# State-space x, B and C of groups 1 to 3: from tokens as the stationary operand to weights as the stationary operand

## The chip, the core and the metric

The kernel runs on one core of one Trainium2 chip. TensorE (PE) multiplies, VectorE (DVE), ScalarE (ACT) and GpSimd (POOL) work on tiles in SBUF and on accumulators in PSUM, and DMA queues (SP's and POOL's here) bring weights in. The metric is the device time of one execution in microseconds (us). The kernel before takes 2125.59 us, the median of three runs from 2124.63 to 2127.35. The profiled execution took 2124.81 us and its span, first to last instruction, is 2122.9 us.

## The reference

Four layers work on 256 tokens of 1024 features. Each layer is a feed-forward block, a mixer, and a second feed-forward block, with a layer norm after each. The mixer of layers 0 and 3 is a state-space one (`mamba2_mixer`); layers 1 and 2 have attention. The part that matters:

```python
def mamba2_mixer(x, w_in, conv_w, conv_b, ...):
    zxbcdt = x @ w_in
    z, xbc, dt = jnp.split(zxbcdt, [SSM_D_INNER, SSM_D_INNER + SSM_CONV_DIM], axis=-1)
    xbc = lax.conv_general_dilated(xbc, conv_w[:, None, :], ..., feature_group_count=SSM_CONV_DIM) + conv_b
    xbc = jax.nn.silu(xbc)
    xs, b_ssm, c_ssm = jnp.split(xbc, [SSM_D_INNER, SSM_D_INNER + G * N], axis=-1)
```

So `x` (2048 features), `B` and `C` (512 each) are projected, go through a convolution of four taps along the tokens, separate for each feature, and through SiLU. There are four groups; a group has 512 features of x, 128 of B and 128 of C, which is 768 features or six blocks of 128.

## The kernel before

The tokens stand in two tiles of 128, t = 0 and t = 1. Each has its own generator (`stream`, inside it `ffn`, `ssm` or `attn`), and the driver at the end of `build` steps them by turns: tile 1 runs two pieces behind tile 0 (`lag_at`, `LAG`). A piece is one block of weights of at most 128 x 2048 numbers, one MB. `fetch` brings it into one of 3 `raw` buffers by SP's queue, `load` splits it into a high half `wh` (ACT, L159) and the rest `wl` (DVE, L160), four instructions of 512 columns on each engine, into one of 5 buffers each. A buffer comes free when the second of the tiles has used its piece.

A product is made of three matmuls (`mm3`, L187, L190, L191): high x high, high x low, low x high. The stationary operand is a 128 x 128 block of the layer's input, transposed and split (`xh`, `xl`, made by `to_T`), and the moving operand is 512 or 256 columns of the weights. So a result stands with tokens on the partitions.

In the state-space mixer the pieces go in the order `SSM_ORDER`: X0, Z0, X1, Z1, O0, X2, Z2, X3, O1, Z3, O2, O3. X is x, B and C of a group, Z its gate, O the output projection. X1, X2 and X3 have three pieces: two with 512 columns of x for half of the 1024 inputs each (`proj512`), one with the 256 columns of B and C (`proj256`). Both tiles multiply every piece. The convolution needs features on the partitions, so `stage_x` copies the result from PSUM to SBUF (ACT, L480), transposes four blocks on PE (`transposes`, L199), and copies them into `xb` (DVE, L482); `stage_bc` does it with two blocks (L492, L199, L494). When tile 1 has done so, `conv` runs for both tiles: on ACT the first tap with the bias (L457), on DVE three taps (L461), on ACT SiLU (L464). `stage_back` then turns x back (L504), scales it (DVE, L509), multiplies C by B (L518) and masks the product (DVE, L521); `stage_off` multiplies by the earlier tile's states (L527), `stage_m` makes the decays on ACT (L540, L541) with a product on DVE (L542), `stage_y` multiplies (L550), `stage_z` is the gate's SiLU (L559). SiLU and the exponential need different function tables on ACT, which ACT_TABLE_LOAD brings in.

The instructions are written in this order, but a scheduler (the Tile layer) reorders them by priority, by when it thinks their operands ready, and by free buffers; `keep_in_program_order` and `high_priority` steer it. PSUM has 8 banks: two each for the tags `acc0`, `acc1`, `gu` (`G`) and `tp` (`T`). Up to the first O piece the projections use `acc0` and `acc1` (`GA`), later ones `gu`, which the products of L527 and L550 use too.

Of the kernel before, what the change touches and what calls it, by code (L numbers as in the profile page):

```python
# [16 lines left out]
S = 256  # L17
# [60 lines left out]
def build(tc, x, wst, ln_g, ln_b, sm_rows, sm_conv, sm_nw, fx_b, out, plan=None):  # L78
# [28 lines left out]

    ident = cpool.tile([128, 128], F32, name="ident")
# [95 lines left out]
    def to_T(st, h):  # L204
        xh = spool.tile([128, KT, 128], FR, name=f"xh{st.t}", bufs=1)
        xl = spool.tile([128, KT, 128], FR, name=f"xl{st.t}", bufs=1)
        for half in range(2):
            tp = transposes(h[:, half * 512:half * 512 + 512], 4)
            sl = slice(half * 4, half * 4 + 4)
            for ins in split(tp.rearrange("p (a b) -> p a b", a=4), xh[:, sl], xl[:, sl]):  # L210
                if opening:
                    tc.keep_in_program_order(ins)
        st.xh, st.xl = xh, xl
# [51 lines left out]
    def proj256(st, ps, w):  # L265
        wh, wl = w
        for k in range(KT):
            mm3(ps[:, :256], st.xh[:, k], st.xl[:, k], wh[:, k * 256:(k + 1) * 256], wl[:, k * 256:(k + 1) * 256],
                k == 0, k == KT - 1)

# [141 lines left out]
    def ssm(st, j):  # L412
# [56 lines left out]
        def frame(g):  # L469
            if t == 0:  # L470
                s.xb[g] = spool.tile([128, 6, S + 3], F32, name="xb", tag="t4", bufs=2)
                s.cv[g] = spool.tile([128, 6, S], F32, name="cv", tag="t4", bufs=2)
                nc.gpsimd.memset(s.xb[g][:, :, 0:3], 0.0)

        def stage_x(g):
            if g:
                frame(g)
            n = 4 if g else 3
            xc = tmp(512, "t2", 4)
            nc.scalar.activation(xc[:, :n * 128], bank.pop(g)[:, :n * 128], AF.Copy)  # L480
            tp = transposes(xc, n)
            nc.vector.tensor_copy(s.xb[g][:, 0:n, 3 + t * 128:131 + t * 128],  # L482
                                  tp[:, :n * 128].rearrange("p (a b) -> p a b", a=n))
            if t == 1:
                conv(g, 0, 4)

        def stage_bc(g):
            if g == 0:
                frame(g)
            n = 2 if g else 3  # L490
            bcs = tmp(128 * n, "t1", 5) if g else tmp(512, "t2", 4)[:, :384]
            nc.scalar.activation(bcs, bank.pop(g if g else "b")[:, :n * 128], AF.Copy)  # L492
            tp = transposes(bcs, n)
            nc.vector.tensor_copy(s.xb[g][:, 6 - n:6, 3 + t * 128:131 + t * 128],  # L494
                                  tp[:, :n * 128].rearrange("p (a b) -> p a b", a=n))
            if t == 1:
                conv(g, 4, 6)
# [85 lines left out]
        for g in range(N_GRP):  # L583
            b = where["X", g, 2 if g else 3]
            at(b - 1 if g else b, stage_x, g)
            at(b if g else 1, stage_bc, g)
# [15 lines left out]
        for i, (kind, g, n) in enumerate(pieces):  # L602
            if kind == "X" and g == 0:
                if n % 2 == 0:
                    ps = bank["b" if n == 0 else 0] = GA(int(n == 0))
            elif (kind == "X" and n != 1) or (kind == "Z" and n == 0):
                ps = bank[g] = GA(int(kind == "Z" or n == 2)) if i < first_o else G()
# [3 lines left out]
            elif kind == "X" and g == 0:  # L611
                proj512(st, ps, n % 2, w, 416 if n < 2 else 384)
            elif kind == "X" and n == 2:
                proj256(st, ps, w)
            else:
                proj512(st, ps, n, w)
            for f, a in post.get(i, ()):
# [284 lines left out]
def pack_ssm(w_in, w_out):  # L902
    P = []
    dn = rows2(w_out)
    for it in SSM_ORDER:
# [5 lines left out]
        elif it[0] == "X":  # L911
            P += cols512(w_in[:, 2048 + g * 512:2048 + (g + 1) * 512])
# [80 lines left out]
```

## Time and profile before

| what | before |
|---|---|
| median of three runs | 2125.59 us (2124.63 to 2127.35) |
| profiled execution | 2124.81 us, span 2122.9 us |
| PE busy | 2099.0 us (99%), 10218 matmuls |
| PE's weight loads (PEld) busy | 1735.6 us (82%), 10218 |
| DVE, ACT, POOL busy | 1461.4 (69%), 1177.0 (55%), 480.9 us (23%) |
| TensorE's granted clock | 0.999 of full speed |

How to read it: a matmul's row is longer than the distance to the next one, since matmuls overlap. What a matmul costs is therefore read from the distance between starts, and what PE waits from the gaps that a row names in brackets. The two state-space mixers stand at about 194 to 364 us and 1736 to 1908 us.

### The profile page before, as it was taken

The page shows a single profiled execution, that of the slowest core. Times are in us where ns is not written, and L with a number is a line of the kernel's source. Part 1 is how long each engine was busy: PE and PEld are TensorE (multiplying, and loading weights), DVE is VectorE, ACT ScalarE, POOL GpSimd, SP SyncE. Part 2 cuts the span into 40 slices and gives each one's busy share as a digit, 9 for nine tenths or more (in the row PEclk, how much of TensorE's full clock was granted, in tenths as well). Part 3 has the DMA queues.
Part 4 walks back from the last instruction along what each step waited for, and adds up shares of the span by engine and source line. Part 5 has one row for each costly group of instructions (what it writes and reads, how often), then busy time and mean ns, then how long its engine had stood idle before and what let it go on. Part 6 is the DMA issues. An engine that isn't in the chain of part 4 may idle for free.

```text
span 2122.9 us, 29645 instructions
## 1 busy us (share of the span) xinstructions
PE 2099.0 (99%) x10218; PEld 1735.6 (82%) x10218; DVE 1461.4 (69%) x2829; ACT 1177.0 (55%) x2453; POOL 480.9 (23%) x871
## 2 busy tenths in 40 slices
PE   8999999999999999999999999999999999999998
PEld 7888878888888888788888888788888888788886
DVE  6557888855765585766675575765575578888565
ACT  5545997544544455544444455544445449975442
POOL 2331000233143210043233300034223310002331
PEclk9999999999999999999999999999999999999999
DMA  9665654666576653476566653376666656446662
GB/s 316 224 229 203 215 171 172 217 232 224 189 256 227 224 201 122 165 235 230 204 245 230 222 193 139 123 247 238 225 221 232 221 205 220 173 161 221 230 227 95
DMA packets 227559, 441.72 MB, mean 208 GB/s; under 512 B 20752, under 2 KB 21072, under 8 KB 227408
## 3 DMA queue, kind: packets, MB, share of 16 engines
q1 hardware_dynamic: 198768, 397.73, 52.5%
q0 software_dynamic: 28640, 42.09, 6.8%
q8 instruction: 80, 1.31, 0.3%
q14 instruction: 71, 0.58, 0.1%
HBM read 417.61 MB, written 22.13 MB: 207 GB/s over the span
## 4 chain that ended last, share of the span: by engine, by line
PE 91%; DVE 4%; ACT 2%; DMA 1%; issue 1%; POOL 0%; SPq 0%; DVEq 0%; ACTq 0%
PE gu L187 16%; PE gu L190 16%; PE gu L191 16%; PE acc L191 9%; PE acc L187 9%; PE acc L190 9%; PE ga L187 3%; PE ga L190 3%; PE ga L191 3%; PE tp L199 3%; DVE wl L160 2%; PE gu L550 1%; DMA raw<-in_w_dram 1%; PE gu L747 1%; DVE cv L461 1%
## 5 line engine op out<-in xcount | busy, mean ns | idle before, releaser
L160 DVE TENSOR_TENSOR wl<-raw,wh 128x512 fp32r<-128x512 f32 (+1 forms) x1412 | 889.1, 680 | 363.1 <-ACT wh L159 361.7
L159 ACT ACTIVATE wh<-raw 128x512 fp32r<-128x512 f32 (+1 forms) x1412 | 778.8, 620 | 511.2 <-PE gu L191 230.0
L187 PE MATMUL gu<-wh,xh 128*128 128x512 f32 (+1 forms) x1600 | 619.4, 387 | 2.7 <-ACT wh L159 1.2
L190 PE MATMUL gu<-wl,xh 128*128 128x512 f32 (+1 forms) x1600 | 618.6, 387 | 0.0
L191 PE MATMUL gu<-wh,xl 128*128 128x512 f32 (+1 forms) x1600 | 618.1, 386 | 0.0
L291 POOL DMA_DIRECT2D aT<-turn x640 | 348.3, 551 | 488.4 <-issue 314.7
L187 PEld LDWEIGHTS gu<-wh,xh 128*128 128x128 f32 x1600 | 301.1, 188 | 65.0 <-ACT wh L159 2.0
L187 PE MATMUL acc<-wh,ah 128*128 128x512 f32 x896 | 352.7, 394 | 0.0
L191 PE MATMUL acc<-wh,al 128*128 128x512 f32 x896 | 351.9, 393 | 0.3 <-DVE al L160 0.3
L190 PE MATMUL acc<-wl,ah 128*128 128x512 f32 x896 | 351.5, 392 | 0.0
L190 PEld LDWEIGHTS gu<-wl,xh 128*128 128x128 f32 x1600 | 301.2, 188 | 60.5 <-DVE wl L160 1.0
L191 PEld LDWEIGHTS gu<-wh,xl 128*128 128x128 f32 x1600 | 301.2, 188 | 59.8 <-DVE xl L160 0.4
L315 ACT ACTIVATE t<-gu 128x256 f32<-128x256 f32 x176 | 67.5, 383 | 267.8 <-PE gu L191 247.2
L317 DVE TENSOR_TENSOR t<-t,gu 128x256 f32<-128x256 f32 x176 | 73.4, 417 | 189.6 <-ACT t L315 189.6
L191 PEld LDWEIGHTS acc<-wh,al 128*128 128x128 f32 x896 | 168.3, 188 | 36.5 <-DVE al L160 2.1
L187 PEld LDWEIGHTS acc<-wh,ah 128*128 128x128 f32 x896 | 168.3, 188 | 35.8 <-issue 1.3
L190 PEld LDWEIGHTS acc<-wl,ah 128*128 128x128 f32 x896 | 168.3, 188 | 34.5 <-issue 1.3
L287 POOL DMA_DIRECT2D turn<-tb x160 | 90.4, 565 | 330.9 <-DVE tb L285 298.5
L187 PE MATMUL ga<-wh,xh 128*128 128x512 f32 (+4 forms) x448 | 159.5, 357 | 0.4 <-ACT xh L159 0.4
L190 PE MATMUL ga<-wl,xh 128*128 128x512 f32 (+4 forms) x448 | 156.8, 351 | 0.0
L191 PE MATMUL ga<-wh,xl 128*128 128x512 f32 (+4 forms) x448 | 155.7, 349 | 0.0
L235 POOL TENSOR_TENSOR rstd<-ve,mhalf 128x1 f32<-128x1 f32 x24 | 22.7, 945 | 441.9 <-DVE ve L233 441.9
(181 smaller groups left out, 1655.5 us busy)
## 6 DMA issues: line engine op xcount, KB each, us to landing
raw<-in_w_dram SPq DMA_DIRECT2D x354, 1024.0 KB, 5.3
turn<-tb POOLq DMA_DIRECT2D x160, 128.0 KB, 3.1
aT<-turn POOLq DMA_DIRECT2D x640, 32.0 KB, 3.9
mt<-cums SPq DMA_DIRECT2D x32, 256.0 KB, 4.2
gb<-in_ln_g_dram SPq DMA_DIRECT2D x12, 512.0 KB, 4.7
gb<-in_ln_b_dram SPq DMA_DIRECT2D x12, 512.0 KB, 5.8
nw<-in_sm_nw_dram SPq DMA_DIRECT2D x8, 256.0 KB, 5.4
h<-in_x_dram SPq DMA_DIRECT2D x4, 256.0 KB, 4.9
```

The lines of the kernel that those rows point to most:

```text
L159: a = nc.scalar.activation(wh, raw, AF.Copy)
L160: return a, nc.vector.tensor_sub(wl, raw, wh.bitcast(F32))
L187: first = nc.tensor.matmul(o, xh, wh, start=start, stop=False)
L190: nc.tensor.matmul(o, xh, wl, start=False, stop=False)
L191: nc.tensor.matmul(o, xl, wh, start=False, stop=stop)
L199: ins = nc.tensor.transpose(tp[:, j * 128:(j + 1) * 128], src[:, j * 128:(j + 1) * 128], ident)
L235: nc.gpsimd.tensor_tensor(rstd, ve, mhalf, op=ALU.pow)
L287: nc.gpsimd.dma_start(dr, b.rearrange("p q k t -> p (q k t)"))
L291: nc.gpsimd.dma_start(aT[32 * q:32 * q + 32].rearrange("p i k t -> p i (k t)"), dv[q])
L315: nc.scalar.activation(sg, gu[:, :256], AF.Silu)
L317: nc.vector.tensor_mul(a, sg, gu[:, 256:])
L461: nc.vector.scalar_tensor_tensor(cv[:, i], xb[:, i, k:k + S], w[:, k:k + 1], cv[:, i], op0=ALU.mult, op1=ALU.add)
```

## The change

For groups 1 to 3 the operands change places. A piece now holds 256 features for all 1024 inputs: two pieces of x and one of B and C per group. `proj_T` takes a 128 x 128 block of the weights as the stationary operand and the 256 tokens of both tiles as the moving one. For this the four tensors `xh0`, `xl0`, `xh1`, `xl1` become slices of one constant tile `x4`, in which the high halves of both tiles stand side by side and the low halves too. The result comes out with features on the partitions and all tokens in a row, so `stage_T` copies it from PSUM straight into `xb` (ACT) and `conv` follows for two blocks at a time. Tile 0 does nothing in these pieces; tile 1 does the whole, at its own place in the order, two pieces behind. Group 0 stays as it was.

```diff
+    x4 = cpool.tile([128, KT, 4, 128], FR, name="x4")
...
     def to_T(st, h):
-        xh = spool.tile([128, KT, 128], FR, name=f"xh{st.t}", bufs=1)
-        xl = spool.tile([128, KT, 128], FR, name=f"xl{st.t}", bufs=1)
+        xh, xl = x4[:, :, st.t], x4[:, :, 2 + st.t]
...
+    def proj_T(ps, w):
+
+        wh, wl = w
+        for f in range(2):
+            o = ps[:, f * S:f * S + S]
+            for k in range(KT):
+                sl = slice(k * 256 + f * 128, k * 256 + f * 128 + 128)
+                nc.tensor.matmul(o, wh[:, sl], x4[:, k, 0:2], start=k == 0, stop=False, skip_group_check=True)
+                nc.tensor.matmul(o, wh[:, sl], x4[:, k, 2:4], start=False, stop=False, skip_group_check=True)
+                nc.tensor.matmul(o, wl[:, sl], x4[:, k, 0:2], start=False, stop=k == KT - 1, skip_group_check=True)
...
         def frame(g):
-            if t == 0:
+            if t == 0 or g:
...
-            n = 4 if g else 3
-            xc = tmp(512, "t2", 4)
-            nc.scalar.activation(xc[:, :n * 128], bank.pop(g)[:, :n * 128], AF.Copy)
-            tp = transposes(xc, n)
-            nc.vector.tensor_copy(s.xb[g][:, 0:n, 3 + t * 128:131 + t * 128],
-                                  tp[:, :n * 128].rearrange("p (a b) -> p a b", a=n))
-            if t == 1:
-                conv(g, 0, 4)
...
+        def stage_T(g, n):
+
+            if n == 0:
                 frame(g)
...
+            nc.scalar.activation(s.xb[g][:, 2 * n:2 * n + 2, 3:3 + S],
+                                 bank.pop((g, n)).rearrange("p (a b) -> p a b", a=2), AF.Copy)
+            conv(g, 2 * n, 2 * n + 2)
...
         for g in range(N_GRP):
             b = where["X", g, 2 if g else 3]
-            at(b - 1 if g else b, stage_x, g)
-            at(b if g else 1, stage_bc, g)
+            if g == 0:
+                at(b, stage_x)
+                at(1, stage_bc)
+            elif t == 1:
+                for n in range(3):
+                    at(b - 2 + n, stage_T, g, n)
...
-            elif kind == "X" and n == 2:
-                proj256(st, ps, w)
-            else:
+            elif kind == "Z":
                 proj512(st, ps, n, w)
+            elif t == 1:
+                ps = bank[g, n] = GA(0) if i < first_o else G()
+                proj_T(ps, w)
...
         elif it[0] == "X":
-            P += cols512(w_in[:, 2048 + g * 512:2048 + (g + 1) * 512])
+            for n in (0, 256):
+                P += cols256(w_in[:, 2048 + g * 512 + n:2048 + g * 512 + n + 256])
```

What the scheduler makes of it is seen in the order of the instructions. Line numbers after the change are a little higher: L279 to L281 are `proj_T`, L189, L192 and L193 are `mm3`, L201 and L519 transposes, L533 is L518 of before, L542 is L527, L161 is the split's high half, L469 and L476 belong to `conv`, L510 is the copy of `stage_T`, L555 and L556 are `stage_m`, and L574 is the gate's SiLU.

First place: PE in the first state-space mixer, where the last piece of X1 (B and C) is multiplied. `tp<-ident,t` are transposes into PSUM, x4 counts four of them. Before:

```order
L191 MATMUL ga<-wh,xl_1935 128x256
L187 MATMUL ga<-wh,xh_1934 128x256
L190 MATMUL ga<-wl,xh_1934 128x256
L191 MATMUL ga<-wh,xl_1935 128x256
L199 MATMUL tp<-ident,t_2484 128x128 x4
L187 MATMUL ga<-wh,xh_1934 128x256
L190 MATMUL ga<-wl,xh_1934 128x256
```

The same place after the change:

```order
L279 MATMUL ga<-x_78,wh 128x256
L280 MATMUL ga<-x_78,wh 128x256
L281 MATMUL ga<-x_78,wl 128x256
L279 MATMUL ga<-x_78,wh 128x256
L280 MATMUL ga<-x_78,wh 128x256
L281 MATMUL ga<-x_78,wl 128x256
L189 MATMUL acc_2617<-wh,ah 128x512
```

The transposes of x and of B and C are gone from PE (36 in each of the two mixers), and the piece runs into the output projection O0; a group's 96 matmuls of both tiles, half of them of 512 and half of 256 columns, have become 144 of 256.

Second place: PE in the first mixer where the output projection O1 begins (`acc`). `tp<-cv` is the product of C and B of group 2, and L527 the product with the earlier states. Before:

```order
L191 MATMUL gu<-wh,xh_1934 128x512
L187 MATMUL gu<-wh,xh_1934 128x512
L190 MATMUL gu<-wl,xh_1934 128x512
L199 MATMUL tp<-ident,t_3175 128x128 x4
L191 MATMUL gu<-wh,xl_1935 128x512
L527 MATMUL gu<-xe,t_3130 128x512
L187 MATMUL acc_2602<-wh,ah 128x512
L190 MATMUL acc_2602<-wl,ah 128x512
L191 MATMUL acc_2602<-wh,al 128x512
```

After:

```order
L189 MATMUL gu<-wh,x_78 128x512
L192 MATMUL gu<-wl,x_78 128x512
L193 MATMUL gu<-wh,x_78 128x512
L189 MATMUL acc_2617<-wh,ah 128x512
L189 MATMUL acc_2762<-wh,ah 128x512
L189 MATMUL acc_2618<-wh,ah 128x512
L189 MATMUL acc_2763<-wh,ah 128x512
L192 MATMUL acc_2617<-wl,ah 128x512
L533 MATMUL tp<-cv 128x128
L519 MATMUL tp<-ident,cv 128x128 x4
```

O1 now begins ahead of the product of C and B, directly behind the gate projection Z2 of tile 1, and its first matmuls are those of both tiles that need only the high halves of the weights; X3, which was multiplied by tile 0 ahead of O1, now follows it.

Third place: ACT in the same stretch. `wh_3134` and `wh_3206` before, `wh_3158` and `wh_3205` after, are the two pieces of O1; `mt` belongs to the decays, `t2` of L559 or L574 to the gate. Before:

```order
L540 ACTIVATE mt_3552<-mt_3552,ncum_2095 128x128
L159 ACTIVATE wh_3134<-raw_3132 128x512 x2
L464 ACT_TABLE_LOAD
L464 ACTIVATE cv_2828<-cv_2828 128x512
L159 ACTIVATE wh_3134<-raw_3132 128x512 x2
L480 ACTIVATE t2_3175<-gu_3026 128x512
L540 ACTIVATE mt_3552<-mt_3552,ncum_2095 128x128 x2
L541 ACT_TABLE_LOAD
L541 ACTIVATE mt_3552<-mt_3552 128x512
L159 ACTIVATE wh_3206<-raw_3204 128x512 x4
L559 ACT_TABLE_LOAD
L559 ACTIVATE t2_3201<-gu_3066 128x512
```

After:

```order
L161 ACTIVATE wh_3105<-raw_3103 128x512 x3
L161 ACTIVATE wh_3158<-raw_3156 128x512 x2
L476 ACT_TABLE_LOAD
L476 ACTIVATE cv_2922<-cv_2922 128x512
L161 ACTIVATE wh_3158<-raw_3156 128x512 x2
L161 ACTIVATE wh_3205<-raw_3203 128x512 x4
L555 ACTIVATE mt_3291<-mt_3291,ncum_2153 128x128 x3
L555 ACTIVATE mt_3611<-mt_3611,ncum_2088 128x128
L556 ACT_TABLE_LOAD
L556 ACTIVATE mt_3291<-mt_3291 128x512
L574 ACT_TABLE_LOAD
L574 ACTIVATE t2_3201<-gu_3102 128x512
```

The splits of O1's two pieces stand closer together, and the gate's SiLU (L574), after which the `gu` bank of the first piece of X3 comes free, stands behind them and behind two table loads. In the whole program the ACT_TABLE_LOADs go from 57 to 61, two more in each mixer. Outside the two mixers the order on every engine is what it was.

## Rows read from the trace of the kernel before

**Rows 1.** The page's first part: busy time of each engine, share of the span and instructions.

```profile
PE 2099.0 (99%) x10218; PEld 1735.6 (82%) x10218; DVE 1461.4 (69%) x2829; ACT 1177.0 (55%) x2453; POOL 480.9 (23%) x871
```

**Rows 2.** The page's fourth part: the chain that ended last, by engine.

```profile
PE 91%; DVE 4%; ACT 2%; DMA 1%; issue 1%; POOL 0%; SPq 0%; DVEq 0%; ACTq 0%
```

**Rows 3.** Busy time in stretches of the first mixer, of a feed-forward block and of the second mixer (us from the span's start; PE, PEld, DVE, ACT, POOL busy with their instructions, granted clock, DMA share, GB/s).

```profile
220.00:320.00 100.00, 97.22 (x542) 82.26 (x541) 87.41 (x178) 97.50 (x196) 3.09 (x7) 1.00 0.55 189
400.00:570.00 170.00, 170.00 (x752) 140.25 (x752) 105.94 (x200) 81.12 (x169) 54.73 (x100) 1.00 0.67 231
1763.00:1863.00 100.00, 97.21 (x543) 82.02 (x542) 87.34 (x175) 97.50 (x195) 3.10 (x7) 1.00 0.54 187
```

**Rows 4.** What PE waited for in the first mixer, 193.86 to 364 us: who waited, for whom, us in total, times, longest. In the second, 1736.5 to 1908 us, the same rows stand without the one of L492.

```profile
PE tp L518 <- ACT cv L464: 1.2, 1, 1.2
PE gu L527 <- DVE t L521: 1.1, 1, 1.1
PE tp L199 <- ACT t L492: 1.0, 1, 1.0
PE gu L187 <- ACT t L559: 0.6, 1, 0.6
PE tp L199 <- DVE t L569: 0.4, 1, 0.4
```

**Rows 5.** Timeline of PE, matmuls of 512 columns: start us, length, instruction. First and last of 25 in an unbroken run.

```profile
184.76 0.40 PE L187 MATMUL acc<-wh,ah 128*128 128x512 f32 x1
...
190.22 0.39 PE L187 MATMUL acc<-wh,ah 128*128 128x512 f32 x1
```

**Rows 6.** The same view, matmuls of 256 columns, first, two in the middle and last of 21; and of 272 columns, first and last of 24.

```profile
290.24 0.28 PE L187 MATMUL gu<-wh,xh 128*128 128x256 f32 x1
290.36 0.28 PE L190 MATMUL gu<-wl,xh 128*128 128x256 f32 x1
...
292.63 0.28 PE L191 MATMUL gu<-wh,xl 128*128 128x256 f32 x1
...
756.85 0.28 PE L187 MATMUL ga<-wh,xh 128*128 128x272 f32 x1
...
759.74 0.29 PE L191 MATMUL ga<-wh,xl 128*128 128x272 f32 x1
```

**Rows 7.** The same view: four transposes among matmuls of 256 columns, and two among matmuls of 512.

```profile
255.99 0.28 PE L191 MATMUL ga<-wh,xl 128*128 128x256 f32 x1
256.11 0.60 PE L199 MATMUL tp<-ident,t 128*128 128x128 f32 x4
256.47 0.37 PE L187 MATMUL ga<-wh,xh 128*128 128x256 f32 x1
256.67 0.28 PE L190 MATMUL ga<-wl,xh 128*128 128x256 f32 x1
...
245.10 0.39 PE L190 MATMUL ga<-wl,xh 128*128 128x512 f32 x1
245.33 0.38 PE L199 MATMUL tp<-ident,t 128*128 128x128 f32 x2
245.47 0.48 PE L191 MATMUL ga<-wh,xl 128*128 128x512 f32 x1
245.78 0.39 PE L187 MATMUL ga<-wh,xh 128*128 128x512 f32 x1
```

**Rows 8.** Timeline of PE's weight loads in the stretch of Rows 6: the load that belongs to its second matmul.

```profile
290.24 0.19 PEld L190 LDWEIGHTS gu<-wl,xh 128*128 128x128 f32 x1
```

**Rows 9.** Groups of ACT's and DVE's instructions in the first mixer: line, engine, operation, out<-in, shapes, count | busy us, mean ns of one | idle before.

```profile
L541 ACT ACT_TABLE_LOAD x9 | 11.5, 1283 | 0.2
...
L480 ACT ACTIVATE t<-gu 128x512 f32<-128x512 f32 x4 | 2.3, 581 | 0.3 <-PE gu L191 0.3
L492 ACT ACTIVATE t<-gu 128x256 f32<-128x256 f32 x4 | 1.5, 377 | 2.5 <-PE gu L191 2.5
...
L482 DVE COPY xb<-tp 128x512 f32<-128x512 f32 x6 | 4.1, 684 | 1.1 <-PE tp L199 1.1
L494 DVE COPY xb<-tp 128x256 f32<-128x256 f32 x6 | 2.5, 418 | 0.1
```

**Rows 10.** Timeline of ACT, and of PE, around PE's longest wait in the first mixer.

```profile
269.69 1.28 ACT L541 ACT_TABLE_LOAD   x1
...
271.63 1.28 ACT L464 ACT_TABLE_LOAD   x1
272.93 0.63 ACT L464 ACTIVATE cv<-cv 128x512 f32<-128x512 f32 x1
...
273.61 0.49 PE L518 MATMUL tp<-cv 128*128 128x128 f32 x2 [1.16 <-ACT cv L464]
```

**Rows 11.** Timeline of ACT in the stretch where X3 begins, with the four parts of a split and four first taps of the convolution in a row.

```profile
302.39 2.18 ACT L159 ACTIVATE wh<-raw 128x512 fp32r<-128x512 f32 x4
304.47 2.07 ACT L457 ACTIVATE cv<-xb,conv 128x256 f32<-128x256 f32 x4
306.56 1.28 ACT L559 ACT_TABLE_LOAD   x1
307.86 0.60 ACT L559 ACTIVATE t<-gu 128x512 f32<-128x512 f32 x1
308.35 0.62 ACT L464 ACTIVATE cv<-cv 128x512 f32<-128x512 f32 x1
```

More of the change, by code (lines that the diff above doesn't have):

```diff
@@ L473, in frame, with stage_x, stage_bc @@
                 nc.gpsimd.memset(s.xb[g][:, :, 0:3], 0.0)
-        def stage_x(g):
-            if g:
-                frame(g)
-            n = 4 if g else 3
-            xc = tmp(512, "t2", 4)
-            nc.scalar.activation(xc[:, :n * 128], bank.pop(g)[:, :n * 128], AF.Copy)
-            tp = transposes(xc, n)
-            nc.vector.tensor_copy(s.xb[g][:, 0:n, 3 + t * 128:131 + t * 128],
-                                  tp[:, :n * 128].rearrange("p (a b) -> p a b", a=n))
-            if t == 1:
-                conv(g, 0, 4)
[L487 to L497, printed above, removed]
+        def stage_x():
+            xc = tmp(512, "t2", 4)
+            nc.scalar.activation(xc[:, :384], bank.pop(0)[:, :384], AF.Copy)
+            tp = transposes(xc, 3)
+            nc.vector.tensor_copy(s.xb[0][:, 0:3, 3 + t * 128:131 + t * 128],
+                                  tp[:, :384].rearrange("p (a b) -> p a b", a=3))
+            if t == 1:
+                conv(0, 0, 4)
+        def stage_bc():
+            frame(0)
+            bcs = tmp(512, "t2", 4)[:, :384]
+            nc.scalar.activation(bcs, bank.pop("b")[:, :384], AF.Copy)
+            tp = transposes(bcs, 3)
+            nc.vector.tensor_copy(s.xb[0][:, 3:6, 3 + t * 128:131 + t * 128],
+                                  tp[:, :384].rearrange("p (a b) -> p a b", a=3))
+            if t == 1:
+                conv(0, 4, 6)
+        def stage_T(g, n):
+            if n == 0:
+                frame(g)
+            nc.scalar.activation(s.xb[g][:, 2 * n:2 * n + 2, 3:3 + S],
+                                 bank.pop((g, n)).rearrange("p (a b) -> p a b", a=2), AF.Copy)
+            conv(g, 2 * n, 2 * n + 2)
         def stage_back(g):
@@ L605, in ssm @@
                     ps = bank["b" if n == 0 else 0] = GA(int(n == 0))
-            elif (kind == "X" and n != 1) or (kind == "Z" and n == 0):
-                ps = bank[g] = GA(int(kind == "Z" or n == 2)) if i < first_o else G()
+            elif kind == "Z" and n == 0:
+                ps = bank[g] = GA(1) if i < first_o else G()
             w = yield
```

## The prediction

> **What bounds the kernel now.** I read the page's first part, then the chain, then the busy time by stretches, and last the waits of PE inside the two mixers that the change touches. PE is busy for 2099.0 of 2122.9 us [rows 1], and the chain that ended last is 91% PE [rows 2]. So matmul time taken away shows in the time one for one, as long as PE is not made to wait instead. The stretches show where that is in doubt. In a feed-forward block PE has no gap and ACT is busy for 81 of 170 us. In the middle of each mixer ACT is busy for 97.5 of 100 us, DVE for 87.4, and PE has gaps of 2.8 us [rows 3]. There ACT is nearly as much the bound as PE, and it stays so only because splits of weights made earlier lie in their buffers. PE's recorded waits add up to 1.2 + 1.1 + 1.0 + 0.6 + 0.4 = 4.3 us in the first mixer and to 3.3 us in the second [rows 4], 7.6 us in all: that is the whole of what a smoother order could give back. [...]
>
> **The transposes that go.** Per mixer three groups, two tiles, four blocks of x and two of B and C: 36, so 72 in all. Their price is read from the starts around a burst. From the matmul at 255.99 us to the one at 256.67 us lie 0.68 us, and two steps of 256 columns account for 0.24 of them, so four transposes cost 0.44 us. From 245.10 to 245.78 us lie 0.68 us, two steps of 512 columns account for 0.455, so two cost 0.225 us [rows 7]. Both give 0.11 us each. 72 x 0.11 = 7.9 us less.
>
> **The matmuls that change shape.** The columns that move are the same, 36864 per group, but they come in 144 matmuls instead of 96. A step of 512 columns is (190.22 - 184.76) / 24 = 0.2275 us [rows 5]; a step of 256 columns is (292.63 - 290.24) / 20 = 0.1195 us [rows 6]. Before, a group takes 48 x 0.2275 + 48 x 0.1195 = 16.66 us; after, 144 x 0.1195 = 17.21 us. That is 0.55 us more per group, and with three groups in two mixers 3.3 us more.
> The trace has no matmul of this form with the weights stationary and both tiles moving, so I bound the step. It can't well be below 0.109 us, near what a transpose costs with its own load [rows 7], nor do I see why it should be above the next larger shape, 272 columns, (759.74 - 756.85) / 23 = 0.126 us [rows 6]. With these, a group takes 15.7 or 18.1 us, and the term is -5.8 or +8.9 us. I take 0.1195 us, since the shape, the number format and one load per matmul are those of that row.
> Every matmul has its own load, so 288 loads come in, less the 72 of the transposes. A load takes 0.19 us; the one that starts at 290.24 us is for the matmul at 290.36 us, and lies beside the matmul that runs from 290.24 us [rows 6, 8]. It is hidden at this step already, so it has no term of its own.
> [...]
>
> **ACT and DVE.** Per group ACT loses two copies of 512 and two of 256 columns, 2 x 0.581 + 2 x 0.377 = 1.92 us, and gets three of 512, 1.74 us [rows 9]; the new copy writes two strided pieces, which DVE's copy into the same tile does at the price of any instruction of 512 columns (0.684 us). DVE loses 2 x 0.684 + 2 x 0.418 = 2.2 us per group [rows 9], 6.6 us per mixer. But the order has two more table loads per mixer at 1.283 us [rows 9]. ACT's sum in a mixer is therefore 2 x 1.28 - 3 x 0.18 = 2.0 us more, while PE's work in it falls by 4.6 / 2 = 2.3 us. All of this lies beside PE, and it counts only where PE waits.
>
> **The waits.** The longest of them, 1.2 and 1.1 us at the product of C and B and behind it, comes after X1: ACT loads the exponential's table at 269.69 us, SiLU's again at 271.63 us, and only then finishes the convolution for which PE waits at 273.61 us [rows 10]. After the change X1's six blocks are convolved two by two as each piece ends, the transposes and DVE's copies no longer stand ahead of them, and the order puts no table load in front of the last SiLU. I expect this wait (2.3 us in each mixer) to shrink or go.
> Against it stands the second place of the order. While tile 0 skips X3, its three pieces hold three of the five weight buffers, so O1's two pieces can be split only when tile 1 is done with the two of Z2, and PE wants them right behind. Tile 1's last matmul of the first piece of Z2 and O1's first matmul lie one piece of 12 matmuls apart, 12 x 0.2275 = 2.7 us, where ACT needs 0.52 us for a first part [rows 11] and DVE, by its copies of 512 columns, 0.68 us [rows 9], if they come to it at once. They come to it behind other work. From the end of X2 to the SiLU that frees X3's bank ACT has ten parts of splits (one of W, then three, four and two), the copy, two first taps, two SiLUs, four decays, three table loads and an exponential. By starts a part of a split takes (304.47 - 302.39) / 4 = 0.52 us, a tap 0.52, SiLU about 0.5 and a table load 1.3 [rows 11]; decays of 128 columns I take at 0.3. That is 5.2 + 0.5 + 1.0 + 1.0 + 1.2 + 3.9 + 0.5 = 13.3 us. PE has from there to X3 four transposes, 24 matmuls of Z2, 27 of O1 and the products of group 2: 0.4 + 5.5 + 6.1 us, and for the products of group 2 an estimate of 26 short steps at 0.11 us [rows 7] and two longer ones at 0.43, 3.8 us: 15.8 us. So PE stays ahead by 2.5 us if ACT enters on time, and at 97.5% busy it will not be on time by some us. I expect 1 to 3 us of new wait per mixer here, about what the other place gives back, so I leave the sum of the waits as it is, with an error of 2.3 us in the whole.
>
> **The sum.** 2124.8 us of the profiled execution (0.8 us under the median) - 7.9 + 3.3 = 2120.2 us. `x4` being one tile for both tokens' tiles costs nothing in this: outside the mixers the order on every engine is unchanged, and inside them tile 1 reads both halves long after both are written.
>
> **Rivals.**
> *The waits go.* ACT and DVE get their work in smaller portions and DVE has 6.6 us less of it, so PE's 7.6 us of waits vanish but for the 1.0 us of L492, which is group 0's. 2120.2 - 6.6 = 2113.6 us. For it: the cause of the longest wait is removed. Against it: ACT has more to do.
> *ACT becomes the bound in the middle of the mixers.* It is busy for 97.5 of 100 us there [rows 3]. If nothing is left of its lead, the stretch lasts as long as ACT's work: 2.0 us longer per mixer, instead of PE's 2.3 us shorter, so 2124.8 + 4.0 = 2128.8 us. The place is the SiLU that frees X3's bank, and the point from which it decides is ACT coming 2.5 us late to the end of X2, plus 2.3 us per mixer before it costs more than the change gains. If O1's splits, late on DVE as well, add two or three us in each mixer, it is 2133 to 2135 us. Against it: PE is busy in the same stretch for 97.2 of 100 us, and ACT has slack before and after it.
> *The new shape costs more.* A step of 0.126 us: 2124.8 - 7.9 + 8.9 = 2125.8 us. Against it: the rows for the same columns.
> *The loads show.* If loads with both tiles moving did not lie beside the matmul ahead, each of the 288 added ones would be paid with its 0.19 us [rows 8]: 55 us, 2124.8 - 7.9 + 55 = 2172 us. Against it: the load at 290.24 us does lie beside one. [...]
> *The change does not do what it says.* The order shows the 72 transposes gone and nothing moved outside the mixers, so all that could undo it is a wait that the order doesn't show, on `x4`, which both tiles of tokens now share: if at each of the twelve blocks PE waited until tile 1's first transposes (0.44 us), a part on ACT (0.52) and one on DVE (0.68) are through [rows 7, 9, 11], that is 1.64 us twelve times, 20 us, 2140 us.
>
> **How the numbers follow.** About 0.2%, 4.25 us, is what a measurement of this kernel can tell from no change, so faster means under 2121.3 us and slower over 2129.8 us. Forecast as summed, 0.50, from 2117.9 to 2122.5 us: 0.29 faster, 0.21 the same. Waits gone, 0.18, faster. ACT the bound, 0.20: 0.08 the same at 2128.8 us, 0.12 slower beyond it. Shape dearer, 0.09, the same. Loads shown 0.01 and waits on `x4` 0.02, slower. That makes faster 0.47, the same 0.38, slower 0.15. The range leaves out about a third of the first rival below (0.06), and above it the last two and half of ACT's slower share (0.09): 2113.0 to 2131.0 us.
>
> **What would show it.** In the profile after, the steps of L279 to L281 at 0.1195 us and 36 transposes fewer in each mixer would confirm the two terms. The waits of PE in the mixers should sum to between 5 and 10 us, without a long one at the product of C and B behind X1, and with one at O1 or at X3's first piece. The forecast is wrong if the steps are above 0.122 us (864 x 2.5 ns, 2.2 us more), if the waits sum to over 12 us or under 4 us, or if any other part of the span changes by more than 1 us.

## The result, and the profile after

The changed kernel takes 2153.49 us (median of four runs, 2151.98 to 2154.38) against 2126.47 us for the kernel before (four runs). The ratio is 1.0129, with an interval from 1.0113 to 1.0145. It is 27 us slower, where 5 us faster was forecast. The profiled execution took 2154.38 us; its span is 2152.5 us, 29.6 us more than before.

The page's first part, kernel after, to be held against [rows 1]:

```profile
PE 2127.4 (99%) x10434; PEld 1746.5 (81%) x10434; DVE 1450.6 (67%) x2805; ACT 1184.7 (55%) x2451; POOL 481.2 (22%) x871
```

PE is as full as before, with 28 us more of busy time. So PE does not wait: its work takes longer. Busy time by stretches, as in [rows 3], kernel after:

```profile
220.00:320.00 100.00, 96.53 (x617) 85.08 (x615) 86.67 (x184) 98.42 (x192) 3.10 (x7) 1.00 0.56 191
400.00:570.00 170.00, 170.00 (x741) 137.72 (x740) 102.22 (x191) 79.51 (x164) 54.73 (x100) 1.00 0.69 233
```

The second row is the one to read. From 400 to 570 us runs a feed-forward block, whose code and order the change leaves alone. PE has no gap in it, before or after, and its clock is at 1.00 both times, but it gets through 741 matmuls where it did 752 [rows 3]. Something makes the same matmul longer. PE's timeline there, first and last of 25 matmuls in an unbroken run, kernel after:

```profile
416.27 0.40 PE L192 MATMUL gu<-wl,x 128*128 128x512 f32 x1
...
421.87 0.40 PE L192 MATMUL gu<-wl,x 128*128 128x512 f32 x1
```

(421.87 - 416.27) / 24 = 0.2333 us from start to start. A run of 25 in the kernel before gives 0.2275 us [rows 5], and in the feed-forward block, by the same view of the kernel before, (420.51 - 415.07) / 24 = 0.2267 us:

```profile
415.07 0.39 PE L191 MATMUL gu<-wh,xl 128*128 128x512 f32 x1
...
420.51 0.39 PE L191 MATMUL gu<-wh,xl 128*128 128x512 f32 x1
```

Groups of matmuls by line and form, kernel after (form, count | busy us, mean ns of one | idle before):

```profile
L192 PE MATMUL gu<-wl,x 128*128 128x512 f32 x1472 | 587.7, 399 | 0.0
L189 PE MATMUL gu<-wh,x 128*128 128x512 f32 x1472 | 582.6, 396 | 1.6 <-ACT wh L161 1.2 <-ACT x L161 0.2
L193 PE MATMUL gu<-wh,x 128*128 128x512 f32 x1472 | 579.9, 394 | 0.0
...
L189 PE MATMUL ga<-wh,x 128*128 128x512 f32 x192 | 78.8, 410 | 0.0
L192 PE MATMUL ga<-wl,x 128*128 128x512 f32 x192 | 78.4, 408 | 0.0
L193 PE MATMUL ga<-wh,x 128*128 128x512 f32 x192 | 77.2, 402 | 0.0
```

3 x (1472 + 192) = 4992 matmuls have `x4` as stationary operand and 512 moving columns. 4992 x (0.2333 - 0.2267) = 33 us. That and the forecast's -4.6 us make 28.4 us, where the spans differ by 29.6 us. The output projections (`acc`, with `ah` and `al` as stationary operands) step at 0.228 us (423.03 to 425.54 us, 11 steps), hardly more than the 0.227 us that they take in the same block of the kernel before.

The parts that the forecast looked at came out near it. PE's steps in `proj_T` (L279 to L281), kernel after, first and last of 28:

```profile
289.55 0.28 PE L281 MATMUL gu<-x,wl 128*128 128x256 f32 x1
...
292.72 0.28 PE L281 MATMUL gu<-x,wl 128*128 128x256 f32 x1
```

That is 3.17 / 27 = 0.1174 us, where 0.1195 us was taken [rows 6]. What PE waited for in the first mixer, kernel after (193.86 to 380 us; who, for whom, us in total, times, longest):

```profile
PE tp L201 <- ACT t L499: 1.4, 1, 1.4
PE acc L192 <- DVE wl L162: 1.0, 1, 1.0
PE gu L542 <- DVE t L536: 0.8, 1, 0.8
PE acc L189 <- ACT t L574: 0.8, 1, 0.8
PE gu L565 <- DVE mt L557: 0.7, 1, 0.7
PE tp L201 <- DVE t L584: 0.2, 1, 0.2
```

4.9 us here, and 4.0 us by the same view in the second mixer: 8.9 us against 7.6 us [rows 4].

### The profile page after: what moved, and what is told of

It is laid out like the page before. It is cut to its first block, busy times and chain, and to the rows that moved or that the text cites. A ratio compares the mean times of both kernels' runs of the same rounds, so it can differ in the third digit from the quotient of the medians.

```text
span 2152.5 us, 30039 instructions
## 1 busy us (share of the span) xinstructions
PE 2127.4 (99%) x10434; PEld 1746.5 (81%) x10434; DVE 1450.6 (67%) x2805; ACT 1184.7 (55%) x2451; POOL 481.2 (22%) x871
## 4 chain that ended last, share of the span: by engine, by line
PE 87%; DVE 5%; ACT 4%; DMA 2%; issue 1%; POOL 0%; SPq 0%; DVEq 0%; ACTq 0%
PE gu L192 16%; PE gu L189 15%; PE gu L193 15%; PE acc L192 9%; PE acc L193 9%; PE acc L189 9%; DVE wl L162 2%; PE ga L189 2%; PE ga L192 2%; PE tp L201 2%; PE ga L193 2%; DMA raw<-in_w_dram 2%; ACT wh L161 1%; PE gu L565 1%; PE gu L767 1%
## 5 line engine op out<-in xcount | busy, mean ns | idle before, releaser
L162 DVE TENSOR_TENSOR wl<-raw,wh 128x512 fp32r<-128x512 f32 (+1 forms) x1412 | 889.3, 682 | 395.8 <-ACT wh L161 394.4
L161 ACT ACTIVATE wh<-raw 128x512 fp32r<-128x512 f32 (+1 forms) x1412 | 778.6, 620 | 526.7 <-PE gu L193 233.0
L192 PE MATMUL gu<-wl,x 128*128 128x512 f32 x1472 | 587.7, 399 | 0.0
L189 PE MATMUL gu<-wh,x 128*128 128x512 f32 x1472 | 582.6, 396 | 1.6 <-ACT wh L161 1.2
L193 PE MATMUL gu<-wh,x 128*128 128x512 f32 x1472 | 579.9, 394 | 0.0
L192 PE MATMUL acc<-wl,ah 128*128 128x512 f32 x896 | 356.2, 398 | 2.0 <-DVE wl L162 2.0
L189 PE MATMUL acc<-wh,ah 128*128 128x512 f32 x896 | 352.1, 395 | 1.6 <-ACT t L574 1.6
L193 PE MATMUL acc<-wh,al 128*128 128x512 f32 x896 | 353.2, 394 | 0.0
L189 PEld LDWEIGHTS gu<-wh,x 128*128 128x128 f32 x1472 | 277.0, 188 | 71.9 <-ACT wh L161 1.6
L193 PEld LDWEIGHTS gu<-wh,x 128*128 128x128 f32 x1472 | 277.1, 188 | 65.9 <-DVE x L162 0.4
L192 PEld LDWEIGHTS gu<-wl,x 128*128 128x128 f32 x1472 | 277.1, 188 | 64.4 <-DVE wl L162 0.5
L189 PEld LDWEIGHTS acc<-wh,ah 128*128 128x128 f32 x896 | 168.8, 188 | 39.5 <-ACT t L574 1.9
L193 PEld LDWEIGHTS acc<-wh,al 128*128 128x128 f32 x896 | 169.0, 189 | 38.0 <-issue 1.6
L192 PEld LDWEIGHTS acc<-wl,ah 128*128 128x128 f32 x896 | 168.9, 188 | 37.6 <-DVE wl L162 2.8
L189 PE MATMUL ga<-wh,x 128*128 128x512 f32 (+4 forms) x384 | 138.7, 362 | 0.4 <-ACT x L161 0.4
L192 PE MATMUL ga<-wl,x 128*128 128x512 f32 (+4 forms) x384 | 136.4, 356 | 0.0
L193 PE MATMUL ga<-wh,x 128*128 128x512 f32 (+4 forms) x384 | 135.0, 353 | 0.0
```

Source lines behind the costliest of these rows:

```text
L161: a = nc.scalar.activation(wh, raw, AF.Copy)
L162: return a, nc.vector.tensor_sub(wl, raw, wh.bitcast(F32))
L189: first = nc.tensor.matmul(o, xh, wh, start=start, stop=False)
L192: nc.tensor.matmul(o, xh, wl, start=False, stop=False)
L193: nc.tensor.matmul(o, xl, wh, start=False, stop=stop)
```

## Experiments: what makes the matmul longer

The change puts `x4` into the pool of constants, which lies first in each partition; `xh0` to `xl1` lay behind the weights. So all that differs in a feed-forward block is where the stationary operand lies, and that it has other strides. Theory A: this makes its matmuls slower. Theory B: the new projection or its order does it in some other way. "Steps" below are read as above, from 25 matmuls of 512 columns in a feed-forward block. The times of e1 to e9, f1, f2 and g1 are of one execution each. Executions of one kernel lie some 5 us apart (2119.31 to 2124.50 us in ten of g2), so differences of 12 us and more are read here, and smaller ones only where more executions stand behind them.

**e1_before_x4**: the kernel before, with the layout alone.

```diff
+    x4 = cpool.tile([128, KT, 4, 128], FR, name="x4")
-        xh = spool.tile([128, KT, 128], FR, name=f"xh{st.t}", bufs=1)
-        xl = spool.tile([128, KT, 128], FR, name=f"xl{st.t}", bufs=1)
+        xh = x4[:, :, st.t]
+        xl = x4[:, :, 2 + st.t]
```

> The kernel before, with the one tile x4 (in the pool of constants) in place of xh0, xl0, xh1, xl1, and nothing else: no proj_T, no piece cut otherwise. Theory A (where x4 lies makes each matmul slower that has it as stationary operand of 512 moving columns): the step goes from 227 to about 233 ns as in the changed kernel; 5280 such matmuls x 6.4 ns = 34 us, so about 2159 us. Theory B (the new projection and its order make PE slower): as before, 2125 to 2127 us.

2156.66 us against 2127.59 us for the kernel before on the same chip, +29 us, with the transposes and the old projection in place. Its steps (PE's timeline, first and last of 25):

```profile
416.39 0.40 PE L187 MATMUL gu<-wh,x 128*128 128x512 f32 x1
...
421.99 0.40 PE L187 MATMUL gu<-wh,x 128*128 128x512 f32 x1
```

0.2333 us. Theory B falls: the loss needs nothing of the new projection.

**e2_after_x4_in_s** and **e3_after_x4_k_inner**: the changed kernel with `x4` in the other pool, and with other strides in the same pool.

```diff
-    x4 = cpool.tile([128, KT, 4, 128], FR, name="x4")
+    x4 = spool.tile([128, KT, 4, 128], FR, name="x4", bufs=1)     # e2
+    x4 = cpool.tile([128, 4, KT, 128], FR, name="x4")             # e3, x4[:, 0:2, k] for x4[:, k, 0:2]
```

> The changed kernel with x4, same shape and strides, allocated in the pool in which xh0 to xl1 lay before (it starts at byte 114656 of the partition instead of 4224; the weights go back to 8160). Theory A1 (the place of x4): 227 ns steps again and the sum of the prediction, about 2120 us. Theory A2 (the stride of x4, 2048 bytes from k to k): stays at about 2153 us. Theory B: stays at about 2153 us.

> The changed kernel with x4 left in the pool of constants but laid out as four runs of 8 blocks (4 x KT x 128 in place of KT x 4 x 128), so that the blocks of one operand lie 512 bytes apart as before. Theory A2 (stride): about 2120 us. Theory A1 (place): stays at about 2153 us. Theory B: stays at about 2153 us.

e2: 2122.05 us, 5.5 us under the kernel before (2127.59). e3: 2154.10 us. The place decides and the stride does not. The feed-forward block of e2 (busy time by stretches) is back at the count of [rows 3]:

```profile
400.00:570.00 170.00, 170.00 (x752) 140.28 (x751) 105.90 (x200) 81.02 (x167) 55.78 (x101) 1.00 0.70 230
```

**e4_before_shift32**: the kernel before, everything behind the first constants 32 bytes further on.

```diff
+    cpool.tile([128, 8], F32, name="pad")
     ident = cpool.tile([128, 128], F32, name="ident")
```

> The kernel before with a pad of 32 bytes ahead of the constants: weights, x and a all move by 32 bytes and start at multiples of 2048 bytes (or 1024 for some a) in place of 32 below. If what counts is the start of an operand against lines of 64 bytes or more by itself, whatever the other operand does, all 512-column steps change, up to 7968 x 6 ns = 48 us, 2173 us. If it counts only against the moving operand, or absolute place counts, nothing changes: 2125 to 2127 us.

2123.02 us, not slower, with steps of 0.2267 us as before. The 32 bytes change where both operands start against multiples of 64 bytes, and the step does not change with them, as long as both move together.

In the compiled program the buffers of the weights start at byte 8160 of a partition before and at 24544 after, 8192 bytes apart; `xh0` starts at 122848 and `x4` at 4224. 122848 - 8160 is a multiple of 2048, 4224 - 24544 is not. The next runs move `x4` against the weights by pads ahead of it and behind it. The order of instructions on the engines is that of the changed kernel in all of them.

**e5_x4_const_2016**, **e6_x4_shift32**, **e7_x4_shift64**, **e9_x4_shift16**:

```diff
-    x4 = cpool.tile([128, KT, 4, 128], FR, name="x4")
+    cpool.tile([128, 472], ...); x4 = cpool.tile(...); cpool.tile([128, 40], ...)              # e5
+    spool.tile([128, 8], ...); x4 = spool.tile(...); spool.tile([128, 504], ...)               # e6; e7: 16 and 496
+    x4 = spool.tile([128, 4100], FR, ...)[:, 4:].rearrange("p (k s c) -> p k s c", k=KT, s=4); spool.tile([128, 504], ...)   # e9
```

> The changed kernel, x4 still in the pool of constants at the low end of the partition, but with 1888 bytes ahead of it and 160 behind: x4 starts at byte 6112, which is 32 below a multiple of 64 as the weights' buffers do (26592); before the pad it started at 4224, a multiple of 64. Theory R (what counts is how the start of the stationary operand lies against that of the moving one, within 64 bytes or a larger power of two): 227 ns steps, 2120 to 2124 us. Theory L (the low end of the partition is slow to read for the load): stays at 2153 us.

> The kernel of e2_after_x4_in_s with x4 moved by 32 bytes (to byte 114688, a multiple of 64, weights unmoved at 32 below one); all behind it moves by 2048. Theory R with 64 bytes: about 233 ns steps again, 2153 us. Theory L, or theory R with a larger unit in which 32 bytes make no difference: 2120 to 2124 us.

> The same with x4 moved by 64 bytes (byte 114720, 32 past a multiple of 64 and 64 past the phase of the weights). Theory R with 64 bytes: 227 ns steps, 2120 to 2124 us. Theory R with 128 bytes or more: about 2153 us. Theory L: 2120 to 2124 us.

> The same with x4 moved by 16 bytes (byte 114672). Theory R with 64 bytes, any difference counts: about 2153 us, or in between if the cost goes with the distance. If only a whole half of the 64 bytes counts, or theory L: 2120 to 2124 us.

e5 took 2120.00, e6 2150.23, e7 2148.82, e9 2126.76 us, against 2127.58 us for the kernel before. Theory L falls with e5, at the low end of the partition and fast, and with e6 and e7, at the high end and slow. 64 bytes as the unit fall with e7. e9 lies between: in one run of 25 its steps are 0.2333 us, from 400 to 562 us most are 0.2268 us. PE's timeline of e6, first and last of 25, for the slow step:

```profile
416.31 0.40 PE L193 MATMUL gu<-wh,x 128*128 128x512 f32 x1
...
421.91 0.40 PE L193 MATMUL gu<-wh,x 128*128 128x512 f32 x1
```

**f1_x4_shift128** and **f2_x4_shift256**: as e6, with pads of 32 and 480, and of 64 and 448 numbers.

> As e7_x4_shift64, with x4 moved by 128 bytes against the phase of the weights (byte 114784). If the phase counts within 128 bytes: 227 ns steps, 2120 to 2124 us. If it counts within 256 or 512 bytes: about 234 ns, 2149 us.

> The same with x4 moved by 256 bytes (byte 114912). If the phase counts within 128 or 256 bytes: 227 ns steps, 2120 to 2124 us. If it counts within 512 bytes (the length of a stationary row, by which all blocks of x4 and a differ and do no harm): about 234 ns, 2149 us.

f1: 2147.70 us, steps of 0.2333 us. f2: 2124.43 us, steps of 0.2267 us (before: 2125.46). At a distance of 128 bytes the loss is still there, at 256 it is gone: the unit is 256 bytes.

Up to here only `x4` had been moved. **g1_weights_160** moves the weights alone, **g2_all_behind_160** all that lies behind the constants; `x4` stays where the change puts it.

```diff
-    x4 = cpool.tile([128, KT, 4, 128], FR, name="x4")
+    x4 = cpool.tile(...); wpool.tile([128, 40], F32, name="pad0", bufs=1)                                            # g2
+    x4 = cpool.tile(...); wpool.tile([128, 40], ...); rpool.tile([128, 472], F32, name="pad1", bufs=1)    # g1
```

> The changed kernel, x4 where the change puts it (byte 4224), and the weights' buffers alone moved by 160 bytes (24704 in place of 24544), so that they are in phase with x4; ah and al keep their phase, which is now 160 bytes off the weights'. If the phase of moving against stationary operand decides, and not the place or phase of x4: steps with x4 at 227 ns, steps of acc with ah and al at about 233 ns, 2688 x 6.5 ns = 17 us above e10, about 2139 us. If it is x4's own start: 2153 us or, with acc slow too, 2170 us.

> The changed kernel, x4 where the change puts it, and everything behind the constants moved by 160 bytes: weights, ah and al, all in phase with x4. If the phase between the operands decides: 227 ns everywhere, time as e10, 2120 to 2124 us, ratio to before about 0.998. If x4's own start decides: 2153 us.

g1: 2138.07 us. PE's timeline of g1, 25 matmuls with `x4`, then 12 of the output projection behind them:

```profile
415.89 0.39 PE L193 MATMUL gu<-wh,x 128*128 128x512 f32 x1
...
421.33 0.39 PE L193 MATMUL gu<-wh,x 128*128 128x512 f32 x1
421.56 0.39 PE L189 MATMUL acc<-wh,ah 128*128 128x512 f32 x1
...
424.14 0.39 PE L193 MATMUL acc<-wh,al 128*128 128x512 f32 x1
```

5.44 / 24 = 0.2267 us with `x4`, which has not moved, and 2.58 / 11 = 0.2345 us with `ah` and `al`, which have not moved against each other either: the slow product has changed places. g2 takes 2122.27 us (ten runs) against 2125.99 us, ratio 0.9978 (0.9968 to 0.9987), with `x4` at its slow byte. In these runs it is the distance of stationary and moving operand, modulo 256 bytes, that the step goes with: 0.2267 us at 0, 0.2345 us at the 96 of `ah` and `al` in g1, 0.2333 us at 160. All buffers of the weights lie in one phase, so it is not shown whether it is the distance to the moving operand of the same matmul or to that of the one ahead. All runs together (start of the stationary operand less start of the moving one, modulo 256; step of 512 columns; time over the kernel before on the same chip):

```
run    x4 - w   a - w   step x4, us   time / before
e2        0       0       0.2267        0.9974
e4        0       0       0.2267        0.9979   (xh0 for x4)
e5        0       0       0.2267        0.9964
f2        0       0       0.2267        0.9995
g2        0       0       0.2267        0.9978
e9       16       0    .2267/.2333      0.9996
e6       32       0       0.2333        1.0106
e7       64       0       0.2333        1.0100
f1      128       0       0.2333        1.0105
after   160       0       0.2333        1.0129
e1      160       0       0.2333        1.0137
e3      160       0       0.2333        1.0125
g1        0      96       0.2267        1.0057
```

**e10_x4_const_2016_timed** is e5 in eleven executions; **e11_ident_2016_timed** also moves the identity matrix, the moving operand of the transposes, into phase with `h` and `t1`. In the compiled program that is about half of the transposes; the others stay out of phase.

```diff
-    ...; x4 = cpool.tile(...); cpool.tile([128, 40], F32, name="pad1")
-    ident = cpool.tile([128, 128], F32, name="ident")
+    ...; x4 = cpool.tile(...)
+    ident = cpool.tile([128, 128], F32, name="ident"); cpool.tile([128, 40], F32, name="pad1")
```

> e5_x4_const_2016 again, timed: the whole change, with x4 in phase with the weights. By the terms of the prediction (-7.9 us of transposes, +3.3 us of matmuls, waits as they were) 4.6 us below the kernel before, ratio 0.9978. If ACT's longer work in the mixers costs what the rival says, 1.0015 or more; if the waits go, 0.995.

> The same, and the identity matrix (moving operand of the transposes) also moved by 160 bytes, to 32 below a multiple of 512, in phase with h, t1 and tb. If phase counts for a transpose as for a matmul of 512 columns, some ns off each of about 400 transposes, 1 to 3 us less than e10; if a transpose is set by its own load (0.11 us against 0.05 us for its 128 columns), no difference.

e10: ratio 0.9983 (0.9974 to 0.9992), e11: 0.9982 (0.9973 to 0.9991). No difference in the time. The 0.05 us for 128 columns agree with the steps of 512 and 256 columns, (0.2275 - 0.1195) / 2 = 0.054 us [rows 5, 6]; that a transpose is set by its own load is not shown by it.

## Experiments: the waits and the clock

With the operands in phase the change is worth 3.5 to 3.7 us. Their profiles show a second thing that the forecast did not have. Busy time by stretches of g2, columns as in [rows 3]:

```profile
275.00:285.00 10.00, 9.64 (x44) 8.52 (x45) 7.67 (x14) 9.94 (x20) 0.55 (x1) 0.66 0.84 238
1815.00:1825.00 10.00, 8.46 (x45) 7.11 (x45) 8.26 (x15) 9.94 (x22) 0.55 (x1) 0.83 0.79 254
```

The granted clock falls to 0.66 and 0.83 in the mean; in the slices of 1 us from 277 to 282 us it is 0.50 of full speed. Before it is 1.00 through both mixers [rows 3]. PE's timeline of g2 shows what comes ahead:

```profile
273.56 1.13 PE L542 MATMUL gu<-xe,t 128*128 128x512 f32 x2 [0.81 <-DVE t L536]
275.36 2.98 PE L565 MATMUL gu<-xdt,mt 128*128 128x64 f32 x16 [0.68 <-DVE mt L557]
...
278.82 0.63 PE L192 MATMUL acc<-wl,ah 128*128 128x512 f32 x1
...
282.23 0.63 PE L189 MATMUL acc<-wh,ah 128*128 128x512 f32 x1
```

Two waits follow each other with only two matmuls (L542) between; PE is busy for 0.45, 0.68 and 0.64 of the three us from 273 to 276 us, and then the clock is down. The nine matmuls from 278.82 us step at 3.41 / 8 = 0.426 us, nearly twice 0.227. In the kernel before the product of L527 has a wait too, but twelve projection matmuls of tile 0's X2 stood between it and L550; tile 0 now skips X2. The kernel before:

```profile
276.25 1.12 PE L527 MATMUL gu<-xe,t 128*128 128x512 f32 x2 [1.05 <-DVE t L521]
276.81 0.79 PE L187 MATMUL gu<-wh,xh 128*128 128x512 f32 x1
...
279.98 1.89 PE L550 MATMUL gu<-xdt,mt 128*128 128x64 f32 x16
```

The fall does not come every time. Six profiles with the changed order (the changed kernel, e2, e5, e10, e11, g2) show the clock by stretches of 5 us, with two mixers each: it falls at this place in 8 of the 12. In the first mixer the two waits are 0.81 and 0.67 us in the changed kernel, where it holds at 1.00, and 0.81 and 0.68 us in g2, where it falls. Each fall withholds 1.7 or 3.4 us of full clock, 3.1 us an execution in the mean of the six. In the profiles of before and e4, with the old order, it stays at 1.00 in both mixers; without a profile three runs of the kernel before, of 2128.78 to 2129.38 us, have a mean clock of 0.996, so a fall there is not ruled out.

**h1_off1_one_piece_later** and **h2_off1_y1_later** place the products of group 1 later, on top of g2.

```diff
-                at(c + 2, stage_off, g)
+                at(c + 2 + (g == 1), stage_off, g)                       # h1 and h2
-            iy = c + 3 + late
+            iy = c + 3 + late + (t == 1 and g == 1)                       # h2
```

> The kernel of g2_all_behind_160 with the product with the earlier states (L542) of group 1 placed one piece later for tile 1; in the order of PE 11 matmuls of O0 and 4 of L565 now stand between the product of C and B and it, in place of 2. Theory W (the waits of 0.8 + 0.7 us there and the fall of the granted clock to 0.50 behind them come from the product standing right behind what it needs): waits under 0.5 us, no clock below 0.9 at 275 to 285 us, and 1.5 us of wait and 1.5 to 3 us of clock less per mixer, 4 to 8 us below g2, 2114 to 2118 us, ratio to before 0.995 to 0.9965. Theory N (the wait only moves on, and the clock falls elsewhere): as g2, 0.998.

> The same with the products of L565 of group 1 also one piece later; 37 matmuls of X2 then stand ahead of most of them. Theory W: as h1. Theory N: as g2. If the later products delay the normalization and with it O1's operands, a new wait at O1 or O2 and a time between.

h1: 2122.04 us, 0.9983 (0.9975 to 0.9992), no better than g2. The wait only moves: 1.9 us at L565 in each mixer. In its profile, of 2119.05 us, the clock is 1.00 from 270 to 290 us and from 1810 to 1830 us. That run and another with a mean clock of 0.999 took 2119.05 and 2119.39 us, the nine with 0.996 to 0.998 2120.40 to 2124.96 us, which would fit falls in some of those; a run's mean clock is no firm guide, though (e10 has 2120.74 us at 0.997 and 2123.33 us at 0.999). h2: 2116.26 us against 2126.41, 0.9950 (0.9937 to 0.9964). It is measured once more on another chip, beside the same placement in the kernel before.

**h2_again** and **h4_before_later**:

> h2 once more, for a profile of an undisturbed execution and a second interval on another chip. If theory W holds as h2's time says: ratio to before 0.994 to 0.9965, no wait over 0.5 us at the products of group 1 (L542, L565), and a granted clock of 1.00 from 270 to 290 us and from 1810 to 1830 us.

> The kernel before with the same two products of group 1 placed one piece later, and no other change. There the longest waits stand at the same products (1.2 + 1.1 us per mixer) with no fall of the clock. If placing them later helps any order: 2.3 us per mixer less, 2121 us, ratio 0.998. If the gain of h2 is bound to the changed order, which has nothing else for PE there: 2125 us, 1.000.

h2: 2114.12 us against 2125.81, 0.9949 (0.9937 to 0.9962). What PE waited for in h2's first mixer:

```profile
PE acc L189 <- ACT t L574: 0.9, 1, 0.9
PE tp L201 <- DVE t L584: 0.4, 2, 0.2
PE tp L201 <- ACT t L499: 0.4, 1, 0.4
PE tp L519 <- DVE xe L524: 0.2, 1, 0.2
```

Busy time by stretches of h2, columns as in [rows 3]:

```profile
220.00:320.00 100.00, 98.72 (x634) 87.03 (x633) 88.80 (x177) 98.63 (x198) 3.28 (x7) 1.00 0.57 199
275.00:285.00 10.00, 9.80 (x74) 8.64 (x73) 9.56 (x18) 9.83 (x24) 0.93 (x1) 1.00 0.73 262
```

No wait at L542 or L565 is left, nor any at O1 (the one at L189 stands at O0), and the clock is 1.00 in these stretches as from 1763 to 1863 us. h4, the same placement without the change: 2119.79 us, 0.9971 (0.9961 to 0.9982). Its waits in the first mixer:

```profile
PE tp L199 <- ACT t L492: 0.8, 1, 0.8
PE gu L187 <- ACT t L559: 0.7, 1, 0.7
PE gu L187 <- DVE sm L567: 0.2, 1, 0.2
PE tp L199 <- DVE t L569: 0.2, 1, 0.2
```

The 2.3 us at the product of C and B [rows 4] are gone there as well. So about 6 us of h2's 11.7 us belong to the placement, which does not need the change. The placement does more than move two products: the profiles have 61 ACT_TABLE_LOADs in g2, 57 in h1 and 53 in h2, 57 in the kernel before and 53 in h4. How much of the gain comes from the shorter work of ACT, and how much from what PE has at hand, no run separates. Between h4 and h2, with the waits of group 1 gone from both and 53 table loads in both, the change is worth 2119.79 - 2114.12 = 5.7 us (medians of eight and of five executions; one of the five took 2119.74 us).

## Why the prediction was wrong

The step that failed is the sentence under the sum: "`x4` being one tile for both tokens' tiles costs nothing in this: outside the mixers the order on every engine is unchanged". The order was unchanged; the addresses were not. 4992 matmuls became 6.6 ns longer, 33 us, against terms of -7.9 and +3.3 us. 2120.2 + 33 = 2153.2 us; the profiled execution took 2154.38 us. The runs without the effect bear the size out: by the ratios 1.0129 and 0.9978 the changed kernel is 32 us slower than g2, which differs from it only in where the operands lie. The forecast named a rival for waits on `x4` and one for a dearer new shape, none for old shapes that become dearer, and the outcome lies 22 us above its range. Its own last test, that no other part of the span should change by more than 1 us, is the one that caught it: the feed-forward blocks did.

**The transposes and the new shape, -7.9 and +3.3 us**: right in their sum within 1 or 2 us, not measured apart. PE has 10434 - 10218 = 216 instructions more, the 288 added matmuls less 72 transposes. With the operands in phase the changed kernel is 3.7 us (g2, 0.9968 to 0.9987) under the kernel before, 3.5 us (e10) by the other way of doing it, and 5.7 us in the pair h4 and h2; forecast were 4.6 us, 0.9978. That g2's ratio is the very 0.9978 is luck in part, since what the clock costs there was not in the sum. The step of 0.1195 us for the new shape was right in phase: h2, first and last of 28, 3.23 / 27 = 0.1196 us.

```profile
278.61 0.28 PE L281 MATMUL gu<-x,wl 128*128 128x256 f32 x1
...
281.84 0.28 PE L281 MATMUL gu<-x,wl 128*128 128x256 f32 x1
```

The loads of `proj_T` take 0.19 us each in the changed kernel, and no row shows an added one beyond the step, so the rivals on loads and on a dearer shape fall.

**The waits**: right in size, and in place but for one. After has 8.9 us where 5 to 10 were expected. The longest, 2.3 us at the product of C and B and behind it, became 0.8 + 0.7 us behind it; a new one of 1.0 us stands at O1 (L192 waiting for DVE's L162), at the lower end of 1 to 3 us. Not forecast was 0.8 us in each mixer at O0 (L189), behind the gate's SiLU.

**The clock**: not in the sum, which has no term for a clock below the 1.00 of [rows 3]. The waits of 1.2 and 1.1 us became 0.8 and 0.7 us, and the clock falls in 8 of 12 mixers, 3.1 us an execution in the mean, about twice the 2 x 0.8 us that the shorter waits gave. The length of the waits does not explain it. Before, 1.2 and 1.1 us [rows 4] had ten short matmuls between them and fourteen of 512 columns behind, and the clock held; now 0.8 and 0.7 us have two between them and sixteen of 64 columns behind. Whether the fall goes with one of these differences is not shown.

**ACT as the bound**: this rival did not come true. ACT has the two added table loads in each mixer, but PE's waits grew by 1.3 us in all, where the rival's 2128.8 us asks for 8.6 us over the sum of 2120.2 us. h2, in which ACT is busy for 98.63 of 100 us and PE loses less than before, is no full test of it, since its placement has eight table loads fewer than the changed kernel.

## What to carry to other kernels

A change that moves a tile in memory can change more than the order: here the step of 4992 matmuls went from 0.2267 to 0.2333 us. Compare the starts of the two operands of the frequent matmuls modulo 256 bytes in both programs, and after the run read first a stretch that the change did not touch: a count of matmuls there that differs at the same busy time says that the step has changed, which no list of waits can show. When one tile of a pair no longer takes part in a stage, look at what it had filled: the twelve matmuls of tile 0 are gone from behind a wait here, and waits of 0.8 and 0.7 us, shorter than the 1.2 and 1.1 us before, came with a clock of 0.50 where it had been 1.00 (g2).

## What the runs showed of the hardware that was not expected

The time of a matmul of 128 x 512 with its load of 128 x 128, both four bytes a number, depends on where its operands start against each other: 0.2267 us if the distance is a multiple of 256 bytes (e2, e4, e5, f2, g2), 0.2333 us at 32, 64, 128 or 160 bytes (e6, e7, f1, the changed kernel), 0.2345 us at 96 (g1, output projection), and at 16 bytes either of the two, mostly the shorter (e9). Distances between 160 and 256 bytes were not tried. By what mechanism is not shown.

With 256 columns being out of phase by 160 bytes is not dearer in `proj_T` but a little cheaper: over all its steps without a wait ahead 0.1197 us in phase (g2) and 0.1179 at 160 bytes (after). For the 864 matmuls of `proj_T` the 1.8 ns would be 1.6 us, an estimate from these two steps; they were not moved by themselves. Where the identity matrix lies made no difference to the time (e10 0.9983, e11 0.9982).

In this kernel the granted clock goes to 0.50 behind waits that are each under 1 us (g2, 0.81 and 0.68 us), in some profiles of one and the same order and not in others (8 of 12 mixers).
